# A hybrid attention and mLSTM layer in split fp32r: the mixer's key and query splits, two weight groups, the output gate's columns and the sums of weight blocks are given other places and engines

## The chip, the cores and the metric

The kernel runs on one core of a Trainium2 chip. The metric is the device time in microseconds (us) of one execution; of several executions the median is taken.

## The reference, cut to what matters

One layer on 256 tokens of width 1024, in fp32:

```python
ada = c @ w_ada + b_ada
shift, scale, gate = jnp.split(ada[:, None, :], 3, axis=-1)
h = _rmsnorm(x, norm_w) * (1 + scale) + shift
(qa, ka, va, za, qm, km, vm, zm, om, ig, fg, ga, gm) = jnp.split(h @ w_in, SPLIT_IDX, axis=-1)
...
ya = (attention(norm(qa), norm(ka), va) * silu(za)) @ w_att_proj
qm, km = jnp.split(silu(causal_dwconv(concat([qm, km]))), 2, axis=-1)
hm = mlstm(qm, km * 256 ** -0.5, vm, ig + b_igate, fg + b_fgate)
hm = sigmoid(om) * hm
hm = _rmsnorm(hm, ml_norm_w)
ym = (merge(hm) * silu(zm)) @ w_ml_proj
y = sigmoid(ga) * ya + sigmoid(gm) * ym
return x + gate * (y @ w_out)
```

The attention has 8 heads of 128, a causal mask and a relative bias. The mLSTM has 4 heads of 256. The projections qa to gm come from one weight w_in of 1024 x 11272; three more weights of 1024 x 1024 follow, and w_ada's third part gives the gate.

## The kernel before, in words

**Products.** TensorE works in fp32r, so each fp32 operand is split into a high part (a rounded copy) and a low part (what the rounding left), and each product is made three times: high by high, high by low, low by high. The weights are 112 groups, each two blocks of 128 rows by 512 columns. `split` makes a group's high part "wh" by a ScalarE copy (L506) and its low part "wl" by a VectorE subtraction (L510; eight early groups have it by GpSimd). Both lie in rings of five buffers, and group g+4 is split in the step in which TensorE multiplies group g.

**Order.** The list `place` (L354 to L366) sets the order of the groups. By number: 0-11 va, 12-19 za, 20-27 qm, 28-35 km, 36-43 w_att_proj ("att"), 44-47 ga's first half, 48-49 zm, then vm's and om's products with zm's and ga's other groups between them, 88-95 gm, 96-103 w_ml_proj ("ml"), 104-111 w_out ("out"). vm and om are made by seven products of blocks each (`PRODUCTS`, P1 P2 P5 P7 P6 P3 P4, the seven-product scheme for 2 x 2 blocks), four groups for one product of both. From P6 on the order before is: 72-75 P6, 76-77 ga's last two groups, 78-81 P3, 82-83 zm's last two groups, 84-87 P4.

**The main loop** (L1104 to L1178) goes through the groups. Step g first evacuates the block product or the "ml" chunk that ended with group g-1, then splits group g+4, then evacuates other chunks that ended, then calls what `at(step, fn)` has put on this step, and then issues the matmuls of group g (L1160 to L1177; block products L1150 to L1152). Each engine works through its own instructions in the order written, so this order decides who waits behind whom. `pump` issues loads on SP's queue into six raw buffers of 1 MB, in the order of the list `loads`, as buffers come free; the weights of the gate (`ada_gate`, four loads of 1 MB, placed by `GSEG`) are in that list, and `gate_acc` (L972) multiplies them by c on VectorE.

**Sums of weight blocks.** Some block products need sums of blocks of w_in. `block_sum` forms them in DRAM: a copy (L761) or an accumulating DMA (L763) on GpSimd's queue, or a plain one on SP's (L765), at the steps `SUM_AT`. The sums of h's blocks are VectorE's (`h_sum`, L793).

**The mixer.** `ml_split(half)` (L881) splits two heads' keys (128 x 512) and queries (128 x 1024): ScalarE copies (L889) and GpSimd subtractions (L890), at steps 44 and 47. `ml_scores` (matmuls L897 and L902, DVE L903, ACT L907, POOL L908) runs at steps 46, 47, 49, 49. `ev_block` evacuates a block product: P2 is copied, P6 has three VectorE steps (L840 to L842), P3 and P4 one (L845, L848); `block_done` then copies a finished block of vm to its high part (ACT L822) and low part (DVE L823), and a finished block of om into its place. After om's P4, two ScalarE sigmoids of 128 x 1024 (L853) finish om. `ml_num` (matmuls L919 to L921, DVE L923, ACT L924 and L926) multiplies each head by it, at steps 89 to 92; `ml_y` (DVE L934 to L937, POOL L938 to L940, DVE L945 four times) is the norm and the factor silu(zm), at 91 and 93; `ml_T` transposes (PE L956, ACT L960, DVE L961) at 94 to 97, and "ml" multiplies the result.

**The output gate.** For the last 256 of out's columns, `gate_columns` (L994) multiplies w_out itself by the gate, on GpSimd, once each at steps 99 to 102; the other columns are multiplied after the product.

Of the kernel before, what the change touches and what calls it, by code (L numbers as in the profile page):

```python
# [16 lines left out]
S = 256  # L17
# [37 lines left out]
SUM_AT = dict(vm=(5, 10, 13, 25, 21, 37, 45, 54), om=(7, 12, 16, 33, 29, 40, 50, 58))  # L55
# [16 lines left out]
def tile_hybrid(ctx: ExitStack, tc: tile.TileContext, x, c, params2, w_row, w_va, ada_mod, ada_gate,  # L72
# [282 lines left out]
    for i, ch in enumerate(chunks):  # L355
# [6 lines left out]
        for j, name in enumerate(("zm", "zm", "ga", "zm", None, "ga", "zm")):  # L362
            if name:
                place += whole[name][:2]
                del whole[name][:2]
            place += [(C[name, j], kp) for name in ("vm", "om") for kp in range(2)]  # L366
    NG = len(place)
# [67 lines left out]
    GSEG = ("qm", "qm", "ga", "zm")  # L435
# [378 lines left out]
    def block_done(name, t, n, src):  # L814
        if name == "om":
            dst = T["parts", name][t, n]
            if src is not dst:
                nc.scalar.copy(dst, src)
            return
# [5 lines left out]
    def ev_block(name, product):  # L825
# [5 lines left out]
        if product == "P1":  # L831
            nc.scalar.mul(x, a, -1.0)
# [14 lines left out]
        elif product == "P4":  # L847
            nc.vector.tensor_tensor(x, a, x, op=OP.subtract)  # L848
            block_done(name, 1, 0, x)
            if name == "om":  # L850
                for n in range(2):
                    cs = T["om"][:, :, 512 * n:512 * n + 512]
                    nc.scalar.activation(cs, cs, AF.Sigmoid)  # L853
# [27 lines left out]
    def ml_split(half):  # L881
        qm, km = T["qm"], T["km"]
        cs = slice(4 * half, 4 * half + 4)
        if half == 0:
            T["kms"] = slot("s6", [128, 2, 2, 4, 128], F32R, "kms")
        qs, ks = slot("s2", [128, 2, 4, S], F32R, "qms"), T["kms"][:, half]
        T["qms"] = qs
        for hl_, src in ((ks, km[:, cs, 0:128]), (qs, qm[:, cs])):
            nc.scalar.copy(hl_[:, 0], src)  # L889
            nc.gpsimd.tensor_tensor(hl_[:, 1], src, hl_[:, 0].bitcast(F32), op=OP.subtract)  # L890
# [98 lines left out]
    def gate_columns(kp):  # L989
# [4 lines left out]
        nc.gpsimd.tensor_tensor(w, w, T["gateb"][:, cs].unsqueeze(1).to_broadcast([128, 2, 256]), op=OP.mult)  # L994
# [52 lines left out]
    for h, step in enumerate((s + 2, s + 3, s + 5, s + 5)):  # L1047
        at(step, ml_scores, h)
    for half in range(2):
        at(s + 3 * half, ml_split, half)  # L1050
    at(start("qm") - 2, gate_init)
    gate_left = {}
    for q, s in enumerate((start("qm"), start("qm") + 2, start("att", 1), start("ga"))):
# [4 lines left out]
    at(start("gm") + 5, gate_read)  # L1058
    for q in range(4):
        at(start("ml") + 3 + q, gate_columns, q)  # L1060
# [7 lines left out]
    for q, name in enumerate(("P5", "P7", "P6", "P3")):  # L1068
        at(start("att") + 1 + 2 * q, h_sum, name)
    for q, name in enumerate(("P5", "P6", "P7", "P3")):  # L1070
        at(start("ga") + q + q // 2, h_high, name)
# [172 lines left out]
```

## Time and profile before

| what | value |
|---|---|
| median of 3 runs | 365.08 us (364.17 to 367.63) |
| the profiled execution | 366.25 us, its span 364.5 us |
| TensorE (PE) busy | 345.9 us, 95% of the span |
| VectorE (DVE) busy | 276.7 us, 76% |
| ScalarE (ACT) busy | 234.6 us, 64% |
| GpSimd (POOL) busy | 98.2 us, 27% |
| mean granted TensorE clock | 0.98 |
| DMA | 100.88 MB, mean 277 GB/s |

The profile is of one execution, and shows it from the first to the last instruction; 1.75 us lie around its span. PE busy counts modelled ends of pipelined matmuls, so a matmul that starts late is seen by its start and by the wait that stands in brackets behind it. "[2.65 <-POOL qms L890]" says that the engine sat idle for 2.65 us, until GpSimd's instruction of line 890 on the tile qms released it. In a table of windows the columns are busy time and number of instructions of PE, PE's weight loads, DVE, ACT and POOL, then the granted clock, the share of DMA and GB/s.

### The profile page before, as it was taken

Reading aid. Unit: us, or ns where it says so; the run is one execution under the profiler, and the core shown is the slowest. Engines: PE = TensorE matmul, PEld = TensorE weight load, DVE = VectorE, ACT = ScalarE, POOL = GpSimd, SP = SyncE. Lnnn points to the kernel's source line nnn. Section 1 sums busy time; section 2 is a strip of 40 time slices with the busy share of each in tenths; the row PEclk is TensorE's granted clock in tenths of the full one; section 3 lists DMA queues with packets and bytes.
Section 4 is the critical chain, followed back from the end, with each engine's and each line's share of the span. In section 5 each row is a group of like instructions: output and inputs, shape, how many; then the busy total and the mean of one; then the engine's idle time right before and its main releaser. Section 6 shows DMA issues by size and latency. Waiting matters only on the chain.

```text
span 364.5 us, 6286 instructions
## 1 busy us (share of the span) xinstructions
PE 345.9 (95%) x2408; PEld 323.6 (89%) x2408; DVE 276.7 (76%) x408; ACT 234.6 (64%) x360; POOL 98.2 (27%) x103
## 2 busy tenths in 40 slices
PE   7999999999999999999988999999999896799996
PEld 7788889999989999999988888988989895699996
DVE  4999987948965798879858685768987545778852
ACT  4768889798866876765562777765967635455410
POOL 4300004851501786568033562000000013121000
PEclk9999999999999999999998999999999999599999
DMA  8999999699999899798999949999985490072011
GB/s 268 417 414 415 416 418 373 148 414 390 304 300 260 279 350 291 289 355 227 281 299 410 341 138 290 296 377 411 420 286 206 150 369 4 0 260 88 2 58 59
DMA packets 35646, 100.88 MB, mean 277 GB/s; under 512 B 3736, under 2 KB 5664, under 8 KB 34848
## 3 DMA queue, kind: packets, MB, share of 16 engines
q1 hardware_dynamic: 30856, 87.36, 64.5%
q0 software_dynamic: 4608, 12.58, 15.3%
q10 hardware_dynamic: 152, 0.53, 0.5%
q8 instruction: 19, 0.31, 0.3%
q14 instruction: 11, 0.09, 0.1%
HBM read 99.21 MB, written 18.03 MB: 322 GB/s over the span
## 4 chain that ended last, share of the span: by engine, by line
PE 64%; issue 9%; DVE 8%; ACT 7%; POOL 6%; DMA 5%; SPq 0%; POOLq 0%; ACTq 0%; DVEq 0%
PE pm L203 12%; PE mm L1176 8%; PE mm L1177 8%; PE mm L1174 8%; DVE wl L510 3%; ACT wh L506 3%; PE mm L1160 3%; PE aux L1151 3%; PE aux L1152 3%; PE aux L1150 3%; PE mm L1169 3%; PE mm L1168 3%; PE mm L1167 3%; DMA raw<-in_w_in_dram 3%; DMA adat<-in_ada_mod_dram 2%
## 5 line engine op out<-in xcount | busy, mean ns | idle before, releaser
L510 DVE TENSOR_TENSOR wl<-raw,wh 128x1024 fp32r<-128x1024 f32 (+1 forms) x104 | 130.5, 1275 | 53.1 <-ACT wh L506 50.1
L506 ACT CAST wh<-raw 128x1024 fp32r<-128x1024 f32 (+1 forms) x112 | 111.5, 1017 | 28.9 <-PE mm L1176 10.4
L1174 PE MATMUL mm<-hTh,wh 128*128 128x256 f32 x320 | 90.4, 283 | 0.0
L1176 PE MATMUL mm<-hTl,wh 128*128 128x256 f32 x320 | 89.3, 279 | 0.0
L1177 PE MATMUL mm<-hTh,wl 128*128 128x256 f32 x320 | 89.3, 279 | 0.0
L1176 PEld LDWEIGHTS mm<-hTl,wh 128*128 128x128 f32 x320 | 60.8, 190 | 0.1
L1174 PEld LDWEIGHTS mm<-hTh,wh 128*128 128x128 f32 x320 | 60.7, 190 | 0.1
L1177 PEld LDWEIGHTS mm<-hTh,wl 128*128 128x128 f32 x320 | 60.6, 189 | 0.0
L1167 PE MATMUL mm<-wh,hTh 128*128 128x344 f32 (+1 forms) x80 | 28.0, 350 | 0.0
L1169 PE MATMUL mm<-wh,hTl 128*128 128x344 f32 (+1 forms) x80 | 27.7, 346 | 0.0
L1168 PE MATMUL mm<-wl,hTh 128*128 128x344 f32 (+1 forms) x80 | 27.7, 346 | 0.0
L188 ACT CAST wrh<-raw 128x512 fp32r<-128x512 f32 (+1 forms) x24 | 18.2, 761 | 8.5 <-DMA raw<-in_w_row_dram 8.5
L510 POOL TENSOR_TENSOR wl<-raw,wh 128x1024 fp32r<-128x1024 f32 x8 | 20.2, 2548 | 10.3 <-ACT wh L506 7.3
L938 POOL TENSOR_SCALAR f<-f 128x4 f32<-128x4 f32 x2 | 0.4, 195 | 80.4 <-DVE f L937 80.4
L193 DVE TENSOR_TENSOR wrl<-raw,wrh 128x512 fp32r<-128x512 f32 (+1 forms) x26 | 20.4, 809 | 0.9 <-ACT wrh L188 0.9
L203 PE MATMUL pm<-wrh,hTh 128*128 128x512 f32 x64 | 19.9, 392 | 0.9 <-ACT hTh L173 0.9
L1176 PE MATMUL mm<-yml,wh 128*128 128x256 f32 x64 | 19.2, 300 | 0.8 <-DVE yml L961 0.8
L203 PE MATMUL pm<-wrh,hTl 128*128 128x512 f32 x64 | 19.9, 391 | 0.0
L1174 PE MATMUL mm<-ymh,wh 128*128 128x256 f32 x64 | 19.3, 301 | 0.0
L1177 PE MATMUL mm<-ymh,wl 128*128 128x256 f32 x64 | 19.1, 298 | 0.0
L203 PE MATMUL pm<-wrl,hTh 128*128 128x512 f32 x64 | 18.9, 393 | 0.0
L1174 PE MATMUL mm<-yah,wh 128*128 128x256 f32 x64 | 17.7, 276 | 0.0
(259 smaller groups left out, 813.5 us busy)
## 6 DMA issues: line engine op xcount, KB each, us to landing
raw<-in_w_in_dram SPq DMA_DIRECT2D x30, 1024.0 KB, 12.1
adat<-in_ada_mod_dram SPq DMA_DIRECT2D x16, 512.0 KB, 8.8
raw<-in_w_va_dram SPq DMA_DIRECT2D x6, 688.0 KB, 9.7
raw<-in_ada_gate_dram SPq DMA_DIRECT2D x4, 1024.0 KB, 9.3
vm_sum<-in_w_in_dram POOLq DMA_DIRECT2D x8, 512.0 KB, 11.8
om_sum<-in_w_in_dram POOLq DMA_DIRECT2D x8, 512.0 KB, 18.2
raw<-in_w_att_proj_dram SPq DMA_DIRECT2D x4, 1024.0 KB, 8.5
raw<-vm_sum SPq DMA_DIRECT2D x8, 512.0 KB, 10.6
```

The costliest lines, as they stand in the source:

```text
L188: copy(wsp[k][0][:, c0:c1], wrow[k][:, c0:c1])
L193: e.tensor_tensor(l[:, cs], wrow[k][:, cs], h[:, cs].bitcast(F32), op=OP.subtract)
L203: nc.tensor.matmul(pm[ch][:, t], a[:, k, t * 128:(t + 1) * 128], b[:, cs], start=k == 0 and i == 0, stop=k == KT - 1 and i == 2)
L506: nc.scalar.copy(h, w)
L510: e.tensor_tensor(l, w, h.bitcast(F32), op=OP.subtract)
L1150: nc.tensor.matmul(o, a[:, k], wh[:, kk], start=ch["fresh"] and k == 0, stop=False, skip_group_check=True)
L1167: nc.tensor.matmul(o, a, wh[:, kk], start=first, stop=False)
L1168: nc.tensor.matmul(o, a, wl[:, kk], start=False, stop=False)
L1169: nc.tensor.matmul(o, b, wh[:, kk], start=False, stop=last)
L1174: nc.tensor.matmul(o, wh[:, kk, cs], sh_[:, k], start=first and i % 2 == 0, stop=False, skip_group_check=True)
L1176: nc.tensor.matmul(o, wh[:, kk, cs], sl_[:, k], start=False, stop=False, skip_group_check=True)
L1177: nc.tensor.matmul(o, wl[:, kk, cs], sh_[:, k], start=False, stop=last and i % 2 == 1, skip_group_check=True)
```

## The change

It has seven parts.

1. `ml_split` becomes `ml_keys` (ScalarE copy, GpSimd low part), called at steps 38 and 41, among att's groups, and `ml_queries` (ScalarE copy, low part by VectorE), called at 44 and 47. The scores are called at 47, 47, 49, 49.
2. In `place`, zm's last two groups go to 76-77, P3 to 78-81, P4 to 82-85, and ga's last two groups to 86-87. Thus eight groups of block products stand in a row. `done("om", 6)` is step 86; `ml_num` is at 88 to 91, `ml_y` at 90 and 92, `ml_T` at 94, 94, 96, 96.
3. Each finished block of om gets its sigmoid at once, 128 x 512 each (`block_done`), in place of a copy or nothing, and the two sigmoids of 128 x 1024 at the end go.
4. `gate_columns` runs on VectorE, a step later (100 to 103); `gate_read` a step later too.
5. `gate_acc` for the third and fourth loads is at 39-40 and 42-43 (before: 40-41 and 44-45), and the fourth of these loads stands ahead of ga's, not of zm's.
6. `SUM_AT`: the sums of weight blocks are formed one to five steps later.
7. The sums and splits of h's blocks are spread differently over the steps 40 to 51.

```diff
--- before.py
+++ after.py
@@ -52,7 +52,7 @@
             ("P6", 1, 0, False), ("P3", (1, 1), 1, False), ("P4", 3, 0, True))
 BLOCK_SUMS = ((0, (0, 0), False), (2, (0, 1), False), (0, (0, 1), True), (2, (1, 1), True), (1, 0, False),
               (1, (1, 1), True), (3, 1, False), (3, (1, 0), True))
-SUM_AT = dict(vm=(5, 10, 13, 25, 21, 37, 45, 54), om=(7, 12, 16, 33, 29, 40, 50, 58))
+SUM_AT = dict(vm=(5, 10, 18, 29, 25, 39, 48, 56), om=(7, 12, 21, 37, 33, 42, 51, 60))
 W_PIECES = ((0, 512), (512, NR), (512, 1024), (1024, NR))
 
 
@@ -359,11 +359,12 @@
             place += [(i, kp) for kp in range(4)]
             continue
         whole = {name: [(C[name, hf], kp) for hf in hfs for kp in range(4)] for name, hfs in (("zm", (0, 1)), ("ga", (1,)))}
-        for j, name in enumerate(("zm", "zm", "ga", "zm", None, "ga", "zm")):
+        for j, name in enumerate(("zm", "zm", "ga", "zm", None, "zm", None)):
             if name:
                 place += whole[name][:2]
                 del whole[name][:2]
             place += [(C[name, j], kp) for name in ("vm", "om") for kp in range(2)]
+        place += whole["ga"]
     NG = len(place)
     G0, GE_ = {}, {}
     for g, (ci, kp) in enumerate(place):
@@ -432,7 +433,7 @@
         return f
 
     NSINGLE = 3
-    GSEG = ("qm", "qm", "ga", "zm")
+    GSEG = ("qm", "qm", "ga", "ga")
     gate_loads = []
     for g, (i, kp) in enumerate(place):
         ch = chunks[i]
@@ -813,9 +814,7 @@
 
     def block_done(name, t, n, src):
         if name == "om":
-            dst = T["parts", name][t, n]
-            if src is not dst:
-                nc.scalar.copy(dst, src)
+            nc.scalar.activation(T["parts", name][t, n], src, AF.Sigmoid)
             return
         hs = slice(2 * n, 2 * n + 2)
         h = T["vm"][:, t, hs, 0:MD]
@@ -829,7 +828,7 @@
         a, b = (bk.rearrange("p (h d) -> p h d", d=MD) for bk in (T["bank", name] * 2)[:2])
         x, y, z = part[1, 0], part[1, 1], part[0, 1]
         if product == "P1":
-            nc.scalar.mul(x, a, -1.0)
+            nc.scalar.activation(x, a, AF.Copy, scale=-1.0)
         elif product == "P2":
             block_done(name, 0, 0, a)
         elif product == "P5":
@@ -847,10 +846,6 @@
         elif product == "P4":
             nc.vector.tensor_tensor(x, a, x, op=OP.subtract)
             block_done(name, 1, 0, x)
-            if name == "om":
-                for n in range(2):
-                    cs = T["om"][:, :, 512 * n:512 * n + 512]
-                    nc.scalar.activation(cs, cs, AF.Sigmoid)
 
     def ev_ga(pt, half):
         T["ga"] = T["att"]
@@ -878,16 +873,18 @@
             nc.vector.tensor_tensor(T["yl"][:, ks[q]], yf[q], T["yh"][:, ks[q]].bitcast(F32), op=OP.subtract)
 
 
-    def ml_split(half):
-        qm, km = T["qm"], T["km"]
-        cs = slice(4 * half, 4 * half + 4)
+    def ml_keys(half):
         if half == 0:
             T["kms"] = slot("s6", [128, 2, 2, 4, 128], F32R, "kms")
-        qs, ks = slot("s2", [128, 2, 4, S], F32R, "qms"), T["kms"][:, half]
+        ks, src = T["kms"][:, half], T["km"][:, 4 * half:4 * half + 4, 0:128]
+        nc.scalar.copy(ks[:, 0], src)
+        nc.gpsimd.tensor_tensor(ks[:, 1], src, ks[:, 0].bitcast(F32), op=OP.subtract)
+
+    def ml_queries(half):
+        qs, src = slot("s2", [128, 2, 4, S], F32R, "qms"), T["qm"][:, 4 * half:4 * half + 4]
         T["qms"] = qs
-        for hl_, src in ((ks, km[:, cs, 0:128]), (qs, qm[:, cs])):
-            nc.scalar.copy(hl_[:, 0], src)
-            nc.gpsimd.tensor_tensor(hl_[:, 1], src, hl_[:, 0].bitcast(F32), op=OP.subtract)
+        nc.scalar.copy(qs[:, 0], src)
+        nc.vector.tensor_tensor(qs[:, 1], src, qs[:, 0].bitcast(F32), op=OP.subtract)
 
     def ml_scores(h):
         qm, km = T["qm"], T["km"]
@@ -991,7 +988,7 @@
         li, ks, cs = raw_of[start("out", 1) + kp]
         cs = slice(cs.start + 256, cs.stop)
         w = rawt[li][:, ks, cs]
-        nc.gpsimd.tensor_tensor(w, w, T["gateb"][:, cs].unsqueeze(1).to_broadcast([128, 2, 256]), op=OP.mult)
+        nc.vector.tensor_tensor(w, w, T["gateb"][:, cs].unsqueeze(1).to_broadcast([128, 2, 256]), op=OP.mult)
 
     def ev_out(pt, c0, n, t):
         cs = slice(c0, c0 + n)
@@ -1044,20 +1041,21 @@
         at(done("za", 0) + 2 + 2 * q, att_av, 2 * q)
         at(done("za", 1) + 1 + q, att_av, 4 + 2 * q)
     s = start("ga")
-    for h, step in enumerate((s + 2, s + 3, s + 5, s + 5)):
+    for h, step in enumerate((s + 3, s + 3, s + 5, s + 5)):
         at(step, ml_scores, h)
     for half in range(2):
-        at(s + 3 * half, ml_split, half)
+        at(s - 6 + 3 * half, ml_keys, half)
+        at(s + 3 * half, ml_queries, half)
     at(start("qm") - 2, gate_init)
     gate_left = {}
-    for q, s in enumerate((start("qm"), start("qm") + 2, start("att", 1), start("ga"))):
+    for q, s in enumerate((start("qm"), start("qm") + 2, start("att") + 3, start("att") + 6)):
         at(s, gate_acc, 2 * q)
         at(s + 1, gate_acc, 2 * q + 1)
         gate_left[s + 1] = gate_loads[q]
     at(start("zm"), gate_write)
-    at(start("gm") + 5, gate_read)
+    at(start("gm") + 6, gate_read)
     for q in range(4):
-        at(start("ml") + 3 + q, gate_columns, q)
+        at(start("ml") + 4 + q, gate_columns, q)
     for name, steps in SUM_AT.items():
         for (i, src, add), step in zip(BLOCK_SUMS, steps):
             for hf in range(2):
@@ -1065,18 +1063,18 @@
     T["A"] = {}
     for kh in range(2):
         at(start("qm", 1) + 1 + 4 * kh, h_full, kh)
-    for q, name in enumerate(("P5", "P7", "P6", "P3")):
-        at(start("att") + 1 + 2 * q, h_sum, name)
-    for q, name in enumerate(("P5", "P6", "P7", "P3")):
-        at(start("ga") + q + q // 2, h_high, name)
-        at(start("ga") + q + q // 2 + 1, h_low, name)
+    for name, step in (("P5", start("att") + 4), ("P7", start("att") + 5), ("P6", start("ga") + 1), ("P3", start("ga") + 2)):
+        at(step, h_sum, name)
+    for name, step in (("P5", start("ga")), ("P7", start("ga") + 1), ("P6", start("ga") + 4), ("P3", start("ga") + 6)):
+        at(step, h_high, name)
+        at(step + 1, h_low, name)
     for hp in range(2):
         s = done("om", 6) + 2 * hp
-        at(s + 1, ml_num, 2 * hp)
-        at(s + 2, ml_num, 2 * hp + 1)
-        at(s + 3, ml_y, hp)
-        at(s + 6, ml_T, 2 * hp)
-        at(s + 7, ml_T, 2 * hp + 1)
+        at(s + 2, ml_num, 2 * hp)
+        at(s + 3, ml_num, 2 * hp + 1)
+        at(s + 4, ml_y, hp)
+        at(s + 8, ml_T, 2 * hp)
+        at(s + 8, ml_T, 2 * hp + 1)
 
     A = HB - 1
     cons = {}
```

**First place: the mixer's splits, on GpSimd and VectorE.** GpSimd's queue before (kms and qms are the keys' and queries' parts; vm_sum and om_sum the sums in DRAM; SD the scores):

```order
L763 DMA om_sum_576<-in_w_in_dram 256x1x512
L890 TENSOR_TENSOR kms<-kmT,kms 128x512
L890 TENSOR_TENSOR qms<-qmT,qms 128x1024
L761 DMA vm_sum_571<-vm_sum_567 16x8192
L908 TENSOR_TENSOR SD<-NM,SD 128x384
L761 DMA vm_sum_572<-vm_sum_568 16x8192
L908 TENSOR_TENSOR SD<-NM,SD 128x384
L890 TENSOR_TENSOR kms<-kmT,kms 128x512
L890 TENSOR_TENSOR qms<-qmT,qms 128x1024
L908 TENSOR_TENSOR SD<-NM,SD 128x384 x2
L761 DMA om_sum_579<-om_sum_575 16x8192
```

Keys and queries of a half are split here in one piece, the second half between the scores. GpSimd's queue after:

```order
L764 DMA om_sum_577<-in_w_in_dram 256x1x512
L881 TENSOR_TENSOR kms<-kmT,kms 128x512
L764 DMA om_sum_578<-in_w_in_dram 256x1x512
L764 DMA vm_sum_567<-in_w_in_dram 256x1x512
L764 DMA vm_sum_568<-in_w_in_dram 256x1x512
L881 TENSOR_TENSOR kms<-kmT,kms 128x512
L764 DMA om_sum_575<-in_w_in_dram 256x1x512
L764 DMA om_sum_576<-in_w_in_dram 256x1x512
L905 TENSOR_TENSOR SD<-NM,SD 128x384 x2
L762 DMA vm_sum_571<-vm_sum_567 16x8192
L905 TENSOR_TENSOR SD<-NM,SD 128x384 x2
```

The queries' rows are gone, and the keys' rows stand among the sums' DMAs, ahead of any score's row. VectorE's queue after, from `ml_queries` of the first half (wl are low parts of weight groups, hsum sums of h's blocks, NM the scores):

```order
L511 TENSOR_TENSOR wl<-raw,wh 128x1024
L887 TENSOR_TENSOR qms<-qmT,qms 128x1024
L511 TENSOR_TENSOR wl<-raw,wh 128x1024
L782 TENSOR_TENSOR hfull<-hfull 128x4x128
L794 TENSOR_TENSOR hsum<-hfull,hsum 128x512
L511 TENSOR_TENSOR wl<-raw,wh 128x1024
L782 TENSOR_TENSOR hfull<-hfull 128x4x128
L794 TENSOR_TENSOR hsum<-hfull,hsum 128x512
L511 TENSOR_TENSOR wl<-raw,wh 128x1024
L900 SCALAR_TENSOR_TENSOR NM<-aux,NM 128x384 x2
L887 TENSOR_TENSOR qms<-qmT,qms 128x1024
L511 TENSOR_TENSOR wl<-raw,wh 128x1024
```

The two rows of qms were in GpSimd's queue before; here each stands between the low parts of two weight groups.

**Second place: ScalarE between P3 of vm and om's last block.** Its queue before (wh are casts of weight groups; vaug is vm's finished block, mm the chunk of ga, zmt silu(zm), omt om):

```order
L858 ACTIVATE mm<-mm 128x1024
L506 CAST wh<-raw 128x1024
L822 CAST vaug<-vmt 128x2x256
L506 CAST wh<-raw 128x1024 x5
L755 ACT_TABLE_LOAD
L755 ACTIVATE zmt<-mm 128x2x512
L506 CAST wh<-raw 128x1024
L822 CAST vaug<-vmt 128x2x256
L506 CAST wh<-raw 128x1024 x2
L853 ACT_TABLE_LOAD
L853 ACTIVATE omt<-omt 128x2x512 x2
L506 CAST wh<-raw 128x1024 x2
```

Ga's sigmoid is first here, then zm's silu, and om's two long sigmoids stand last. After:

```order
L756 ACTIVATE zmt<-mm 128x2x512
L507 CAST wh<-raw 128x1024
L821 CAST vaug<-vmt 128x2x256
L507 CAST wh<-raw 128x1024 x2
L817 ACT_TABLE_LOAD
L817 ACTIVATE omt<-omt 128x512
L507 CAST wh<-raw 128x1024 x2
L821 CAST vaug<-vmt 128x2x256
L507 CAST wh<-raw 128x1024 x2
L817 ACTIVATE omt<-omt 128x512
L507 CAST wh<-raw 128x1024 x3
L853 ACTIVATE mm<-mm 128x1024
```

The long sigmoids are gone; a short one of one block of om stands behind two casts, twice (L817; one more, of P6's block, stands three casts ahead of this piece), zm's silu is first, and ga's sigmoid (L853 there) last.

**Third place: VectorE in "ml", beside out's first groups.** Its queue before (yf and yl are y and its low part):

```order
L875 TENSOR_TENSOR yf<-yf,attT 128x512
L878 TENSOR_TENSOR yl<-yf,yh 128x512 x2
L510 TENSOR_TENSOR wl<-raw,wh 128x1024 x4
L874 TENSOR_TENSOR yf<-mm,gmt 128x512
L875 TENSOR_TENSOR yf<-yf,attT 128x512
L874 TENSOR_TENSOR yf<-mm,gmt 128x512
L875 TENSOR_TENSOR yf<-yf,attT 128x512
L878 TENSOR_TENSOR yl<-yf,yh 128x512 x2
```

The low parts of four groups stand in one piece. After:

```order
L870 TENSOR_TENSOR yf<-yf,attT 128x512
L873 TENSOR_TENSOR yl<-yf,yh 128x512 x2
L511 TENSOR_TENSOR wl<-raw,wh 128x1024
L991 TENSOR_TENSOR raw<-raw,gateb 128x2x256
L511 TENSOR_TENSOR wl<-raw,wh 128x1024
L991 TENSOR_TENSOR raw<-raw,gateb 128x2x256
L511 TENSOR_TENSOR wl<-raw,wh 128x1024
L991 TENSOR_TENSOR raw<-raw,gateb 128x2x256
L511 TENSOR_TENSOR wl<-raw,wh 128x1024
L991 TENSOR_TENSOR raw<-raw,gateb 128x2x256
L869 TENSOR_TENSOR yf<-mm,gmt 128x512
```

The four rows of L991, GpSimd's L994 before, stand one behind each low part.

## What the change does to the time: a prediction

> **What bounds the kernel now.** I read the busy times first, then PE's waits, then windows of 10 us, then the timelines of the windows in which PE is not full.
>
> ```profile
> span 364.5 us, 6286 instructions
> PE 345.9 (95%) x2408; PEld 323.6 (89%) x2408; DVE 276.7 (76%) x408; ACT 234.6 (64%) x360; POOL 98.2 (27%) x103
> ```
>
> PE is the bound nearly everywhere; a change that leaves its work alone can win only what PE waits. The list of PE's waits (total, times, longest):
>
> ```profile
> PE aux L956 <- DVE omt L945: 5.1, 2, 3.8
> PE aux L902 <- POOL qms L890: 3.5, 2, 2.7
> PE aux L919 <- ACT den L924: 1.2, 1, 1.2
> PE aux L645 <- ACT GE L623: 0.8, 1, 0.8
> ```
>
> The first two are at places that the change touches. The windows tell what follows each wait (busy PE, its loads, DVE, ACT, POOL; granted clock, DMA share, GB/s):
>
> ```profile
> 190.00:200.00 10.00, 7.35 (x51) 7.20 (x50) 8.19 (x8) 3.81 (x5) 4.73 (x5) 0.83 1.05 409
> 200.00:210.00 10.00, 9.17 (x58) 8.11 (x57) 6.48 (x7) 7.22 (x9) 4.60 (x3) 1.00 0.89 329
> 210.00:220.00 10.00, 10.00 (x45) 8.28 (x45) 8.04 (x9) 7.96 (x10) 5.53 (x7) 1.00 0.55 188
> 240.00:250.00 10.00, 10.00 (x46) 8.29 (x45) 6.74 (x6) 6.62 (x8) 0.00 (x0) 1.00 1.04 409
> 280.00:290.00 10.00, 8.81 (x74) 8.57 (x74) 5.29 (x8) 7.30 (x13) 0.00 (x0) 1.00 0.24 73
> 300.00:310.00 10.00, 6.17 (x53) 5.98 (x52) 5.31 (x10) 5.36 (x13) 3.07 (x5) 0.93 0.05 19
> 310.00:320.00 10.00, 7.92 (x39) 7.35 (x40) 7.89 (x11) 4.51 (x8) 0.99 (x1) 0.55 0.00 0
> 330.00:340.00 10.00, 10.00 (x88) 10.00 (x87) 7.70 (x10) 4.92 (x6) 0.00 (x0) 1.00 0.01 3
> ```
>
> Both waits are followed by a lower clock (0.83, 0.55), so each costs more than itself. From 210 to 280 PE is full: nothing is to be won there, but something can be lost.
>
> **Part 1, keys and queries.** The scores' place:
>
> ```profile
> 185.80 1.05 ACT L506 CAST wh<-raw 128x1024 fp32r<-128x1024 f32 x1 [3.39 <-DMA raw<-in_w_in_dram]
> 188.35 2.09 POOL L890 TENSOR_TENSOR kms<-kmT,kms 128x512 fp32r<-128x512 f32 x1 [17.05 <-ACT kms L889]
> 190.41 2.35 POOL L890 TENSOR_TENSOR qms<-qmT,qms 128x1024 fp32r<-128x1024 f32 x1
> 190.72 3.11 DVE L510 TENSOR_TENSOR wl<-raw,wh 128x1024 fp32r<-128x1024 f32 x1 [1.41 <-ACT wh L506]
> 195.57 1.21 DVE L510 TENSOR_TENSOR wl<-raw,wh 128x1024 fp32r<-128x1024 f32 x1
> 189.79 0.36 PE L902 MATMUL aux<-qms,kms 128*128 128x256 f32 x1
> 192.81 1.43 PE L902 MATMUL aux<-qms,kms 128*128 128x256 f32 x5 [2.65 <-POOL qms L890]
> 195.96 0.32 PE L1174 MATMUL mm<-hTh,wh 128*128 128x256 f32 x1
> 205.91 0.86 PE L902 MATMUL aux<-qms,kms 128*128 128x256 f32 x5 [0.83 <-POOL qms L890]
> ```
>
> PE starts the second matmul 192.81 - 189.79 - 0.11 = 2.9 us late and then runs at half clock until 195.96, which loses half of 3.15, 1.5 more. In the new order the keys are split six steps earlier, so POOL's 2.09 and 2.35 are off this path; the queries' low part is a VectorE subtraction of 128x1024, 1.21 by the row of L510. It ends near 190, and the scores, one step later, are wanted at 192.1: the wait and its clock go (4.4). The second wait, where the shared buffer is read until the first two heads' scores end, falls from 0.83 to an estimated 0.4, and 0.3 of slow spacing at the first goes: 5.1 in all, of which I keep **5.0**. The row at 190.72 shows a VectorE subtraction stretched from 1.21 to 3.11 beside POOL's; the keys' two will now stretch one each among att's groups. Low parts stand well ahead of PE there (the one of 190.72 is group 49's, whose products come only after the scores of 205.91), so this costs nothing; without that cover it would cost 1.9 each.
>
> What is late next is the DMA. A cast there waits for a load:
>
> ```profile
> 241.37 1.05 ACT L506 CAST wh<-raw 128x1024 fp32r<-128x1024 f32 x1 [1.69 <-DMA raw<-om_sum]
> 242.45 1.23 DVE L510 TENSOR_TENSOR wl<-raw,wh 128x1024 fp32r<-128x1024 f32 x1 [1.51 <-ACT wh L506]
> 247.47 0.39 PE L1150 MATMUL aux<-wh,hsum 128*128 128x512 f32 x1
> ```
>
> From this low part's end (243.67) to its use are 3.8 us; a PE that is 5.0 earlier needs landings that are 1.2 earlier at least, and then has no cover left. In 200 to 220 the share is 0.89 and 0.55 since loads waited for buffers behind the stall: 1.1 + 4.5 = 5.6 us of full DMA stand free and are used when the stall goes. Part 6 brings 1 MB of om's sums into the stretch (an estimated 2.6 us at the 409 GB/s of window 190), and part 5 takes a gate load of 1 MB out of it. If these cancel, all 5.0 arrive, and that I take; if the sums cost their 2.6 and the load had been hidden, 2.4 arrive, and the range keeps that.
>
> **Parts 2 and 3, the eight block groups in a row.** The rows of now for what will stand between:
>
> ```profile
> 260.13 0.68 DVE L842 TENSOR_TENSOR omt<-omt 128x512 f32<-128x512 f32 x1
> 267.11 0.62 ACT L822 CAST vaug<-vmt 128x512 fp32r<-128x512 f32 x1 [2.74 <-DVE vmt L845]
> 267.64 4.84 ACT L506 CAST wh<-raw 128x1024 fp32r<-128x1024 f32 x5
> 272.50 1.28 ACT L755 ACT_TABLE_LOAD   x1
> 273.79 1.03 ACT L755 ACTIVATE zmt<-mm 128x1024 f32<-128x1024 f32 x1
> 276.27 0.28 PE L1174 MATMUL mm<-hTh,wh 128*128 128x256 f32 x1
> 277.64 0.62 ACT L822 CAST vaug<-vmt 128x512 fp32r<-128x512 f32 x1 [1.89 <-DVE vmt L848]
> ```
>
> The times are on the clock of before; stage 1 is taken off at the end. In the new order the sigmoid of om's P6 block stands ahead of the cast of group 80 and waits for VectorE's third step, which ends at 260.8. From there ScalarE does nine casts up to group 88's (9 x 0.97 = 8.7), two sigmoids and two vaug casts of 128x512 (0.6 each, 2.4), two table loads (2.6) and the silu (1.0): 14.7. Twice it waits for VectorE (2.74 and 1.89 now), 4.6, and a low part follows (1.2): 260.8 + 14.7 + 4.6 + 1.2 = 281.3 for group 88, which starts at 276.27 now. Setting both queues in program order by hand gives 281.9, since VectorE too falls behind; I take **281.9, 5.6 later**. Were none of the waits to occur, it would be 276.1, nothing later: the bounds are 0 and 5.6. The table loads stay as many as they were.
>
> The mixer after it:
>
> ```profile
> 297.15 1.67 DVE L945 SCALAR_TENSOR_TENSOR omt<-omt,f,zmt 128x256 f32<-128x256 f32 x4 [1.73 <-POOL f L940]
> 308.38 3.68 DVE L945 SCALAR_TENSOR_TENSOR omt<-omt,f,zmt 128x256 f32<-128x256 f32 x4 [1.70 <-POOL f L940]
> 308.33 2.66 POOL L994 TENSOR_TENSOR raw<-raw,gateb 128x512 f32<-128x512 f32 x2
> 310.02 0.45 PE L956 MATMUL aux<-ident,omt 128*128 128x128 f32 x1 [3.85 <-DVE omt L945]
> 311.72 0.90 PE L956 MATMUL aux<-ident,omt 128*128 128x128 f32 x3 [1.26 <-DVE omt L945]
> 327.74 0.28 PE L1174 MATMUL mm<-ymh,wh 128*128 128x256 f32 x1
> ```
>
> L945's second set takes 3.68 beside POOL's gate columns and 1.67 without; it ends 308.38 + 3.68 = 312.06, 35.8 after step 88 begins. In the new order every piece of the mixer stands one step nearer to step 88 (a group of 2.85 and a head's eight matmuls, some 1 us: 3.9) and the columns are gone from beside it (2.0): 35.8 - 5.9 = 29.9, so it ends at 281.9 + 29.9 = 311.8. The last transposes follow at once, in place of 311.72 with PE idle for 3.85 before. In the new order PE has spent its 5.6 already, so it arrives near 310 and waits about 1.5; then two weight groups' low parts stand ahead of yml in VectorE (2 x 1.2), and the products wait 2.1; the third group waits 1.1 for the next yml. "ml" has its second chunk at about 326.6 instead of 327.74: **1.1 won** out of all that, since the waits are moved rather than removed.
>
> I count no loss of clock for the new waits. The wait of L919, 1.2 us near 288, left the clock at 1.00 (window 280); the one of 2.65 did not, and mine are up to 2.1. Half clock for one stretch like that of 192.81 would cost 1.5, which the range holds.
>
> The Trainium skill, "TensorE: Matmul & The Clock Gate", Part 1, has the clock fall to one half only after an idle window of about 3.4 us. The row at 192.81 shows a wait of 2.65 to be enough, so the measurement decides; by the rule alone the sum would be the same, and the fourth rival below would need longer breaks than by the row.
>
> **Part 4, gate columns by VectorE.** The nearest row, two inputs in SBUF and 128x512:
>
> ```profile
> 194.96 0.68 DVE L793 TENSOR_TENSOR hsum<-hfull,hsum 128x512 fp32r<-128x512 f32 x1
> ```
>
> 4 x 0.68 = 2.7 us more on VectorE where it has 7.70 of 10 (window 330). PE is full there, with low parts some 8 us ahead, and these hide it: 0 to 0.8, taken 0.1.
>
> **Parts 5 to 7** move DMA issues on POOL's and SP's queues past each other and VectorE's small work among att's groups. None of it stands on PE's path in the rows above. One early wait, L645's of 0.8, may go or stay with the sums' DMAs that moved, which the trace of before does not tell: 0 to 0.9 with its spacing, and I take 0.5.
>
> **Sum.** 5.0 + 1.1 - 0.1 + 0.5 = 6.5. Against the profiled execution's 366.25 (span 364.5 and 1.75 around it): 359.75. The median is 365.08, 1.2 lower, which gives 358.6. Forecast: the middle, **359.2**.
>
> **Rivals.**
> - The DMA is the bound in 230 to 250 (share 1.04, casts on landings) and only 2.4 of the 5.0 arrive: 361.8. For it: the row at 241.37 and the sums that move into this stretch. Against: the free 5.6.
> - The eight groups cost little. ScalarE's two waits fall into the time in which it waits for buffers anyway; if group 88 starts 4.4 earlier than I say, everything behind it does: 354.8. For it: the bound of 276.1. Against: sigmoid and casts stand in order behind VectorE.
> - The change does not do what it says: the queries' cast stands behind the cast of group 48, which sat 3.39 for its load before. If that load is 3 us later, since the gate's fourth load is ahead of it, the queries come near 193 again, and the wait with its clock stays: 359.2 + 4.4 = 363.6.
> - Slower: the clock. It halves wherever PE breaks for more than some 2.7 us. If the break near group 84 and the one near 312 each do what the one at 310 did (clock 0.55 in 310 to 320, half speed from about 309 to 319), each costs 5 more: 369.2. It decides from a single break of 2.65; my largest is 2.1. For it: two breaks sum to 5.6 in a short stretch; against: they come in four or five pieces.
>
> **Chances.** Forecast 0.50, DMA 0.20, cheap groups 0.14, queries late 0.09, clock 0.07. The forecast's own range is 357 to 361.4. 1% of 365.08, about what a measurement of this kernel can tell from no change, ends at 361.43 and 368.73. Faster: nearly all of the forecast (0.47), the cheap groups (0.14) and the better quarter of the DMA case (0.05), 0.66. Within: the rest of these two (0.03 and 0.15), late queries (0.09), a mild clock (0.01), 0.28. Slower: 0.06. The range of 354.5 to 364.5 leaves out the clock and the tails, under 0.2.
>
> **What would show it.** Right: no wait of L902 on qms above 0.5, clock 1.00 in the windows from 185 to 205, group 49 five us earlier; new short waits of PE on wl or wh around om's P3 and P4; L956's wait on omt below 2; L945's both sets at 1.7. Wrong: casts that wait for DMA longer than 1.7 near 235 to 250 (first rival), no PE wait from P6 to gm (second), L902 still waiting over 2 (third), a clock under 0.9 in 255 to 285 (fourth).

## The result, and the profile after

The changed kernel takes 369.96 us in the median of 12 runs (367.65 to 371.63), the kernel before 365.38 (364.17 to 367.63): ratio 1.0118, 95% interval 1.0089 to 1.0146. It is slower by 4.6 us; 359.2 was forecast. The profiled execution took 367.65, the fastest of its twelve, so the traces differ by 1.4 us where the medians differ by 4.6.

The page after, and its list of PE's waits (engine, line and tile, who released it; total, times, longest):

```profile
span 365.8 us, 6273 instructions
PE 348.2 (95%) x2408; PEld 322.5 (88%) x2408; DVE 276.5 (76%) x414; ACT 234.5 (64%) x361; POOL 88.5 (24%) x97
```

```profile
PE aux L1148 <- ACT wh L507: 4.9, 2, 4.2
PE aux L1149 <- DVE wl L511: 3.0, 4, 0.8
PE mm L1174 <- DVE yml L958: 2.0, 1, 2.0
PE warm L232 <- POOL ident masks.py:199: 1.4, 1, 1.4
PE aux L953 <- DVE omt L942: 1.3, 2, 0.9
```

The two waits at which the change was aimed are gone or small: L899 (L902 before) does not appear, and L953 (L956 before) fell from 5.1 to 1.3. In their place PE waits for high and low parts of weights at block products. The scores of the first pair of heads now run without a break, and group 47 follows at once:

```profile
190.31 0.60 PE L894 MATMUL aux<-qmT,kmT 128*128 128x128 f32 x4
190.67 0.95 PE L899 MATMUL aux<-qms,kms 128*128 128x256 f32 x6
191.46 0.61 PE L894 MATMUL aux<-qmT,kmT 128*128 128x128 f32 x4
191.82 0.96 PE L899 MATMUL aux<-qms,kms 128*128 128x256 f32 x6
192.62 0.28 PE L1172 MATMUL mm<-hTh,wh 128*128 128x256 f32 x1
```

The loss starts at group 64, the first of om's P5 (the experiments' expectations call it om's P2, but P2 is groups 58 and 59; P5 is om's first product that needs a sum of weight blocks). PE, ScalarE and SP's queue there:

```profile
232.33 0.57 PE L1148 MATMUL aux<-wh,hsum 128*128 128x512 f32 x1 [4.19 <-ACT wh L507]
233.59 0.80 PE L1149 MATMUL aux<-wl,hsum 128*128 128x512 f32 x1 [0.69 <-DVE wl L511]
234.18 0.63 PE L1150 MATMUL aux<-wh,hsum 128*128 128x512 f32 x1
...
240.14 0.39 PE L1165 MATMUL mm<-wh,hTh 128*128 128x512 f32 x1
```

```profile
231.23 1.04 ACT L507 CAST wh<-raw 128x1024 fp32r<-128x1024 f32 x1 [8.04 <-DMA raw<-om_sum]
234.00 1.05 ACT L507 CAST wh<-raw 128x1024 fp32r<-128x1024 f32 x1 [1.73 <-DMA raw<-om_sum]
```

```profile
203.09 13.52 SPq L429 DMA_DIRECT2D raw<-om_sum  x2
```

PE's wait was put down to ScalarE's cast, but the cast itself had waited 8.04 us for a load of om's sums: one step further back stands the DMA. That load's two issues alone held SP's queue for 13.5 us, and its halves landed at 231.2 and 233.9; in the trace of before they were issued at 209.8 and landed at 218.2 and 219.5. After the wait the same matmuls last 0.63 instead of 0.39: the granted clock was halved until about 240 (0.66 on the mean of 230 to 240). Windows of after that tell where the DMA (share and GB/s are the last two columns) was idle and where it was full:

```profile
100.00:110.00 10.00, 10.00 (x83) 9.63 (x83) 6.68 (x19) 7.37 (x15) 0.00 (x0) 1.00 0.34 122
190.00:200.00 10.00, 10.00 (x77) 9.51 (x76) 7.45 (x8) 6.19 (x8) 2.48 (x3) 1.00 1.08 317
200.00:210.00 10.00, 10.00 (x48) 8.38 (x47) 8.45 (x9) 8.24 (x13) 4.96 (x7) 1.00 1.04 410
210.00:220.00 10.00, 10.00 (x47) 8.32 (x47) 6.46 (x7) 7.46 (x8) 1.94 (x2) 1.00 1.06 203
230.00:240.00 10.00, 6.70 (x15) 4.17 (x16) 4.16 (x4) 4.87 (x6) 0.00 (x0) 0.66 1.08 320
```

And the row of before for the first of them:

```profile
100.00:110.00 10.00, 9.22 (x76) 8.79 (x75) 5.94 (x22) 6.83 (x14) 0.00 (x0) 1.00 1.08 302
```

The DMA idled for two thirds of the window at 100 (share 0.34), where it had been full, and it was full from 190 on, where the windows at 200 and 210 had 0.89 and 0.55 before.

The start of PE's first matmul of a group, less its start in the trace of before, tells stage by stage what a kernel has won (minus) or lost. The later experiments stand in the same table (part numbers as in the section on the change). Some 0.7 to 1.0 us of each column stand already at group 8, near 72 us, ahead of anything that the change moves, so they belong to the trace of before; what counts is how a column changes downwards.

| group | place | after | part 1 only | parts 1, 4 | parts 1, 3, 4 | parts 1, 2, 4 | parts 1, 4, 2 MB less | after, 2 MB less |
|---|---|---|---|---|---|---|---|---|
| 44 | ga, before the scores | -1.85 | -0.97 | +0.92 | -0.67 | -0.75 | -0.71 | -1.53 |
| 63 | just before om's P5 | -7.25 | -6.37 | -4.16 | -6.08 | -6.07 | -6.11 | -6.94 |
| 67 | behind om's P5 | +1.53 | -6.37 | -4.16 | -6.08 | -4.45 | -6.11 | -6.43 |
| 78 | vm's P3 | +1.32 | -4.79 | -4.16 | -3.99 | -2.38 | -6.11 | -4.02 |
| 88 | gm | +8.62 | -2.84 | -2.55 | +1.21 | +2.20 | -6.12 | +5.94 |
| 100 | "ml", second chunk | +1.80 | -2.56 | -4.03 | -0.70 | -4.18 | -9.05 | -1.53 |

After wins 5.4 us between groups 44 and 63, loses 8.8 by group 67 and 7.1 more by group 88, and wins 6.8 back by group 100. In the columns with part 2, 1.1 us of the row of group 88 is no loss: the first head's numerators stand ahead of that group there and behind it in the kernel before:

```profile
283.82 0.28 PE L916 MATMUL aux<-vaug,SD 128*128 128x258 f32 x1
...
284.89 0.28 PE L1172 MATMUL mm<-hTh,wh 128*128 128x256 f32 x1
```

### The profile page after: what moved, and what is told of

It reads as the page before. It is cut to its first block, busy times and chain, and to the rows that moved or that the text cites. A ratio compares the mean times of both kernels' runs of the same rounds, so it can differ in the third digit from the quotient of the medians.

```text
span 365.8 us, 6273 instructions
## 1 busy us (share of the span) xinstructions
PE 348.2 (95%) x2408; PEld 322.5 (88%) x2408; DVE 276.5 (76%) x414; ACT 234.5 (64%) x361; POOL 88.5 (24%) x97
## 4 chain that ended last, share of the span: by engine, by line
PE 75%; DVE 7%; ACT 6%; DMA 6%; issue 3%; SPq 2%; POOL 1%; POOLq 0%; ACTq 0%; DVEq 0%
PE pm L203 12%; PE mm L1174 11%; PE mm L1172 11%; PE mm L1175 11%; DMA raw<-in_w_in_dram 6%; DVE wl L511 4%; ACT wh L507 4%; PE mm L1166 4%; PE mm L1167 4%; PE mm L1165 3%; PE mm L1158 3%; SPq L429 2%; PE aux L1148 1%; PE aux L1149 1%; PE aux L1150 1%
## 5 line engine op out<-in xcount | busy, mean ns | idle before, releaser
L511 DVE TENSOR_TENSOR wl<-raw,wh 128x1024 fp32r<-128x1024 f32 (+1 forms) x104 | 127.8, 1249 | 52.3 <-ACT wh L507 51.9
```

The source lines that it names most:

```text
L511: e.tensor_tensor(l, w, h.bitcast(F32), op=OP.subtract)
```

## The experiments

Each kernel was timed in turn with the kernel before on the same chip; ratios are to that kernel, with 95% intervals. Its median was 365.65 us in the first group (four kernels), 365.23 in the second (four), 366.58 in the third (four) and 366.49 in the last (three), so ratios are compared and not times.

### Which part loses: sums, gate, place, or part 1

**Sums back.**

```diff
-SUM_AT = dict(vm=(5, 10, 18, 29, 25, 39, 48, 56), om=(7, 12, 21, 37, 33, 42, 51, 60))
+SUM_AT = dict(vm=(5, 10, 13, 25, 21, 37, 45, 54), om=(7, 12, 16, 33, 29, 40, 50, 58))
```

> The changed kernel with the sums of weight blocks (SUM_AT) at the steps of before. In the changed profile PE has won 7.2 us by group 63, then waits 4.35 us at group 64 (om's P2) for a load of sums that was issued at 210.8 and landed at 233.9, the clock halves, and 9 us are lost by group 67. Theory A (the later copies and adds of the sums are bunched in front of that load): with the sums back, the wait at group 64 goes and most of the 9 us come back, 361 to 363 us, and no wait of PE for L507 over 1 us. Theory B (the DMA is full whatever the order of the sums, since PE asks 7 us earlier): the wait stays near 4 and the time near 369 to 370. Theory C (the loss is in the eight block groups in a row, 7 us there): 369 to 370 as well, with the wait at group 64 gone only if A holds too.

365.19 us, ratio 0.9992 (0.9966 to 1.0017). The wait at group 64 is gone and 1.26% came back, 4.6 us, less than theory A said: the second pair of scores now waits, 2.9 us by the starts of its matmuls, its queries behind a cast that waited for a load, and group 49 has 2.64 won instead of 7.25. So part 6 costs as much as the whole difference between the two kernels, and the DMA shows itself at another place. The kernel is still some 6 us above the forecast of 359.2, though, and from group 78 to 88 it loses 9.7 (-2.86 to +6.81): part 6 is not all that the forecast missed.

**Gate back.**

```diff
-    GSEG = ("qm", "qm", "ga", "ga")
+    GSEG = ("qm", "qm", "ga", "zm")
...
-    for q, s in enumerate((start("qm"), start("qm") + 2, start("att") + 3, start("att") + 6)):
+    for q, s in enumerate((start("qm"), start("qm") + 2, start("att", 1), start("ga"))):
```

> The changed kernel with the gate's third and fourth loads and their products (GSEG, gate_acc) where they were before. Theory A: this load is not what holds om's P2 back; the wait at group 64 stays over 3 us, 368 to 371 us. Theory B (DMA full before 200): the 1 MB load comes back into the full stretch, and the wait at group 64 grows by up to 2.6 us, 371 to 373 us.

369.12 us, 1.0098 (1.0070 to 1.0126): no different from the changed kernel. The late load is now zm's behind om's P5 (PE waits 5.2 us there, at 240.8). Both gate and sums back gave 366.21, 0.9988 (0.9961 to 1.0015), the same as the sums alone:

> The changed kernel with the sums' steps and the gate's loads and products (parts 5 and 6) of before. With the sums alone back 365.2 us, and PE then waits 2.9 us at the second pair of scores, behind loads that the gate's load has pushed back. Theory A2 (what counts is which transfers stand ahead of a load that PE needs): that wait goes, and 362 to 363 us come out. If the gate's load does not matter: 365 us, with the wait still there.

The second pair of scores waited there too, so the gate's load is not what delays it; part 5 moves nothing that can be measured. This kernel has parts 1 to 4 and 7, and will be compared below.

**Place back.** `place`, `ml_num`, `ml_y` and `ml_T` as before, all else changed.

> The changed kernel with the order of the groups and the mixer's steps of before (part 2 undone); the om sigmoids by block, the queries, the gate and the sums stay changed. Theory A and B: the loss at group 64 is upstream and stays; the eight groups' 7 us go, but the waits of the mixer's transposes (5 to 7 us) come back, so the sum moves by under 1.5 us: 368.5 to 371.5. Theory C: the place is what costs, and 365 or less comes out.

369.57 us, 1.0122 (1.0092 to 1.0152). With the sums back as well:

> The changed kernel with the sums and the order of the groups of before (parts 2 and 6 undone). With the sums back 365.2 us. If the eight groups in a row cost as much as the mixer's earlier steps win, as the two traces so far say (7 lost to group 88, 7 won back by group 96), 364.5 to 366 us; if the place is a loss by itself, under 363.5 us.

365.94 us, 1.0013 (0.9985 to 1.0040). Both pairs agree: as the change has it, with part 3, the place costs about what the mixer wins by it.

**Part 1 alone on the kernel before.** `ml_keys` and `ml_queries` with their steps, and the scores at 47, 47, 49, 49.

> The kernel before with part 1 alone: keys split in att by ScalarE and GpSimd, queries' low part by VectorE, scores at 47, 47, 49, 49. Theory A: no wait of the scores, full clock, 5 us won at group 49, and 2.4 to 5 of them kept to the end, 360.5 to 363 us. Theory B: the DMA takes it all back between 215 and 250, with a wait of PE for a load of sums over 3 us: 365 us or more.

363.61 us, 0.9945 (0.9924 to 0.9967). Between groups 44 and 63 it wins 5.4 us, and over half of what stood at group 63 is gone by group 88 (-6.37 to -2.84). The gain of 2.0 us (1.2 to 2.8 by the interval) is near the prediction's lower bound of 2.4, and the time is just above the 360.5 to 363 expected.

### Which of the sums, and why

**Last steps back, first steps back, third steps back.** "First" are the first that the change moved: each list's third to sixth entries; "third" is the third entry alone. In the changed kernel's `SUM_AT`:

```diff
-SUM_AT = dict(vm=(5, 10, 18, 29, 25, 39, 48, 56), om=(7, 12, 21, 37, 33, 42, 51, 60))
+SUM_AT = dict(vm=(5, 10, 18, 29, 25, 39, 45, 54), om=(7, 12, 21, 37, 33, 42, 50, 58))
...
+SUM_AT = dict(vm=(5, 10, 13, 25, 21, 37, 48, 56), om=(7, 12, 16, 33, 29, 40, 51, 60))
...
+SUM_AT = dict(vm=(5, 10, 13, 29, 25, 39, 48, 56), om=(7, 12, 16, 37, 33, 42, 51, 60))
```

> The changed kernel with only the last two steps of SUM_AT of each of vm and om back (copies and adds of the fourth sums; 45, 54 and 50, 58). Putting all sums back won 4.8 us. If the bunching of those last copies and adds (206 to 221) in front of om's P2 load is the cause, this alone brings 365 to 366.5 us and no wait at group 64. If the earlier sums that moved into 170 to 200 are the cause, 369 to 370 us.

> The counterpart: only the third to sixth steps of SUM_AT back, the last two stay late. Bunching of the last copies: 369 to 370 us, the wait at group 64 stays. Work pushed into 170 to 200: 365 to 366.5 us.

> The changed kernel with only the third step of SUM_AT of vm and om back (18 to 13, 21 to 16): the only sums that could fill the DMA near 100 us. If the idle DMA there is the cause of the wait at om's P2, the share of 100 to 110 returns to over 1 and 364.5 to 366 us come out. If it is the fourth to sixth steps that bring work into 170 to 200, 369 us or more.

Last steps back: 368.88, 1.0090 (1.0056 to 1.0124). First ones back: 364.86, 0.9974 (0.9952 to 0.9995). My first story, that the last copies and adds bunch up in front of om's P5, fell: moving them back is worth nothing clear of the noise, and the third to sixth steps are worth the rest. The third steps alone, back: 371.64, 1.0139 (1.0114 to 1.0164), so the idle time near 105 us is not it either, by itself. The windows of this last kernel show why:

```profile
100.00:110.00 10.00, 9.16 (x75) 8.72 (x74) 5.21 (x19) 7.34 (x15) 0.00 (x0) 1.00 1.07 301
140.00:150.00 10.00, 10.00 (x87) 10.00 (x86) 8.71 (x16) 6.53 (x11) 7.23 (x4) 1.00 0.33 122
```

The DMA is full again at 100 to 110 and idles at 140 to 150 instead (0.95 before): the hole has moved to the next late sums. Summing the shares of the windows from 50 to 200 gives the DMA time used by then: 14.7 windows before, 14.5 with the first sums back, 14.4 with all back, but 14.0 in the changed kernel, with the last ones back and with the third ones back. The three that are 0.4 to 0.7 windows short, 4 to 7 us of DMA, are the slow ones. The same sum over the other traces agrees: 14.0 with the gate back, with the place back and with part 6 alone, all slow, and 14.4 to 14.7 in every kernel that has all sums at the old steps. The share is a rough measure (it goes over 1), but the GB/s of the same windows say so too: 47.0 MB before, 45.3 in the changed kernel. How such a hole comes about is told by GpSimd's queue, where the third sums are issued. Before:

```profile
92.11 1.97 POOL L763 DMA_DIRECT2D vm_sum<-in_w_in_dram  x2
94.12 0.31 POOL L615 MEMSET GE<- 36x256 f32 x1
94.37 2.10 POOL L763 DMA_DIRECT2D om_sum<-in_w_in_dram  x2
```

And after:

```profile
91.25 0.31 POOL L616 MEMSET GE<- 36x256 f32 x1
110.85 1.31 POOL L709 TENSOR_TENSOR yal<-yf,yah 128x512 fp32r<-128x512 f32 x1 [19.29 <-ACT yah L708]
112.11 1.28 POOL L764 DMA_DIRECT2D vm_sum<-in_w_in_dram  x1
...
124.53 1.01 POOL L764 DMA_DIRECT2D om_sum<-in_w_in_dram  x1
```

Five steps later in the program means behind a subtraction that waits 19 us for attention's result. The four accumulating DMAs, 2 MB, start 20 to 34 us later, and nothing else fills the DMA.

**Part 6 alone on the kernel before.** The same two lines of `SUM_AT`.

> The kernel before with part 6 alone, the sums' later steps. The DMA then idles near 105 us, as in the changed kernel (share 0.34 in 100 to 110, against 1.08). If that work is missed later whatever PE's pace, om's P2 load lands near 232 as in the changed kernel, and PE, which wants it at 235 here, waits little: 365 to 367 us. If the loss comes from the sums alone, 369 to 370 us. If the sums' later steps help (the early wait of 0.9 near 105 goes), 364 us.

369.77 us, 1.0088 (1.0060 to 1.0115). PE, without the win at the scores, still loses 3.1 us from group 70 to 74 and 2 more by group 82. So the sums cost by themselves; the earlier PE of the changed kernel is not needed for it. The early wait of 0.9 near 105 does go (group 20 starts 0.9 earlier against group 12), as the prediction hoped for.

**Less to load.** The third and fourth loads of the gate's weights and their products are left out, on the changed kernel and on parts 1 and 4, so that half of the output gate is missing:

```diff
-    GSEG = ("qm", "qm", "ga", "ga")
+    GSEG = ("qm", "qm")
...
-    for q, s in enumerate((start("qm"), start("qm") + 2, start("att") + 3, start("att") + 6)):
+    for q, s in enumerate((start("qm"), start("qm") + 2)):
```

> The changed kernel without the third and fourth loads of the gate's weights and their four products, so half of the gate's vector stays zero: 2 MB less for the DMA, 4.9 us at the 410 GB/s of its full windows, and 5 us less for VectorE near 165 to 180. Theory A2 (the DMA is a second bound; the share lost at 100 to 110 is missed in 170 to 235): the wait at group 64 (4.35 and its half clock) goes for the most part, and 362 to 365 us come out. Rival (the order of issues on the queues holds om's P2 load back, not the amount): 368 to 370 us, with the wait still over 3.

> Parts 1 and 4 on the kernel before, with the same 2 MB left out. That kernel (361.7) kept 4.2 of the 5.1 us from the scores until group 80, and lost 1.5 at groups 80 to 82. If its loss is the DMA's, it goes, 359 to 360.5 us. If the DMA no longer binds there, no change: 361.7, or 0.5 less from VectorE.

364.86 us, 0.9953 (0.9927 to 0.9978), and 359.69, 0.9798 (0.9741 to 0.9855). On the changed kernel the wait at group 64 is gone (-6.94 at group 63, -6.43 at 67) with the order of all other issues untouched. On parts 1 and 4 the whole win stays up to group 88 (-6.11, -6.12). Its window behind the scores:

```profile
200.00:210.00 10.00, 10.00 (x53) 8.57 (x52) 8.50 (x9) 7.10 (x10) 5.53 (x7) 1.00 0.47 131
```

There is room again. This takes VectorE's four products away as well, which the run cannot tell apart; but the waits that went were for loads. So what holds PE from 230 on is the DMA work that is still left to do by then. Whether the order of the issues near 200 matters besides is not shown.

### The parts that can win

**Gate columns by VectorE, with part 1.**

```diff
-        nc.gpsimd.tensor_tensor(w, w, T["gateb"][:, cs].unsqueeze(1).to_broadcast([128, 2, 256]), op=OP.mult)
+        nc.vector.tensor_tensor(w, w, T["gateb"][:, cs].unsqueeze(1).to_broadcast([128, 2, 256]), op=OP.mult)
...
-        at(start("ml") + 3 + q, gate_columns, q)
+        at(start("ml") + 4 + q, gate_columns, q)
```

> The kernel before with part 1 and the gate's columns by VectorE one step later (part 4). Part 1 alone gave 363.6 us, with L945's second set still stretched beside GpSimd (3.7 against 1.7). If the stretch lies on the path, the transposes come 2 us earlier and 361.5 us comes out; the 2.7 us more on VectorE are hidden. If they are not hidden, 363.6 us or more.

361.68 us, 0.9904 (0.9867 to 0.9941), as expected (1.5 us better than part 1 alone, but the two intervals overlap). L945's second set takes 1.67 in this trace and 3.68 in that of part 1 alone.

**Om's sigmoids by block on top.** Part 3, as in the section on the change.

> The kernel before with parts 1, 3 and 4: queries by VectorE, om's sigmoids by block, gate columns by VectorE. Parts 1 and 4 alone gave 361.7 us, with PE still waiting 1.9 for the den of the first numerators behind om's two long sigmoids, and 2.2 for the last transposes. If the long sigmoids hold the mixer up, 359.5 to 361 us; if the short sigmoids between the casts cost PE as much around P6 to P4, 361.7 or more.

366.09 us, 0.9992 (0.9970 to 1.0014): not faster but 0.9% slower. ScalarE with it and, behind, without it:

```profile
253.98 1.99 ACT L506 CAST wh<-raw 128x1024 fp32r<-128x1024 f32 x2
259.38 0.63 ACT L816 ACTIVATE omt<-omt 128x512 f32<-128x512 f32 x1 [3.41 <-DVE omt L840]
259.91 2.92 ACT L506 CAST wh<-raw 128x1024 fp32r<-128x1024 f32 x3
```

```profile
253.65 4.84 ACT L506 CAST wh<-raw 128x1024 fp32r<-128x1024 f32 x5
```

ScalarE idles for 3.41 us ahead of the sigmoid of om's P6 block, which needs VectorE's three steps on that block, and three casts wait behind it that the other kernel does in one go with the two ahead. PE waits 1.87 us for the first of them, and 3.3 us are lost at groups 78 to 82 (-3.99 to +0.89, against -4.16 to -2.56 without).

**The place, without part 3.** Parts 1, 4 and 2.

> Parts 1, 4 and 2 on the kernel before: the new order of the groups and of the mixer's steps, but om's sigmoids as before, at the end. Part 3 on top of parts 1 and 4 cost 3.5 us at groups 80 to 82, where om's P6 sigmoid stands ahead of a cast. If that sigmoid is also what made the eight groups in a row dear (7 us), the mixer's earlier steps now win: 358.5 to 360.5 us. If the evacuations of vm between the casts do it, 361.7 or more.

361.53 us, 0.9865 (0.9805 to 0.9924), the lowest ratio of the kernels that compute the whole layer; its interval overlaps that of parts 1 and 4. The gain over those is smaller than expected: it loses more to loads on the way (3.7 by group 78), then 4.6 in the eight groups instead of 7.3 (3.5 and 6.2 without the numerators' 1.1), and wins 6.4 back in the mixer.

Set beside the kernel with both gate and sums back (parts 1 to 4 and 7, 0.9988), this one (parts 1, 2 and 4) is 1.23% faster, 4.5 us. So part 3, perhaps with part 7, costs about that much on the new place; on the old one part 3 alone costs 3.2 (0.9992 against 0.9904).

## Why the prediction was wrong, point by point

**The step that failed is the one on the DMA in part 1**: "Part 6 brings 1 MB of om's sums into the stretch ... and part 5 takes a gate load of 1 MB out of it. If these cancel, all 5.0 arrive." I counted one pair of sums by its new step and did not look at where the other late sums came to stand in GpSimd's queue. Parts 5 to 7 were put down with "None of it stands on PE's path". In fact the sums left 4 to 7 us of DMA unused before 200, and from 170 on the DMA is a second bound: PE had 7.25 won at group 63 and was at +1.53 at group 67. The 5.6 us of free DMA that the prediction found in 200 to 220 could cover the win at the scores or the lost time, not both; the shares there are 1.04 and 1.06 after the change. The term was -5.0 and should have been about +3.4 (-5.4 at the scores, +8.8 behind). The last bound I gave, 2.4 kept, is close to what part 1 keeps when the sums stay where they were (2.0).

**A second step failed: "stage 1 is taken off at the end", in parts 2 and 3.** It takes the cost of the eight groups to be the same for a PE that arrives earlier. Part 6 is worth 4.6 of the 10.8 us between forecast and result; with it undone 365.2 come out, not 359. The second pair of scores, which then waits for a load again, takes 2.9. The table shows another place where the rest goes: with 2 MB less to load, PE is 6.43 ahead at group 67 and still +5.94 at group 88, a loss of 11.3 without the numerators' 1.1, where the changed kernel loses 6.0. So of the 8 us that the late load cost at group 67, only 2.7 are left at group 88. What makes the stretch dear for an early PE is in part the sigmoids of part 3, 3.2 to 4.5 us by the two comparisons above; how the rest divides is open.

**The DMA rival had the place and not the size.** It took the bound as "only 2.4 of the 5.0 arrive"; it should have been a loss, from a count of the DMA's free time along the whole way.

**Part 1 was right**: no wait at the scores, full clock, 5.4 us from group 44 to 63 where 5.0 to 5.1 was forecast.

**Parts 2 and 3 came out near the forecast in the changed kernel itself, in part by luck.** Step 88 begins at 283.82 with the numerators, so from group 78 on 6.2 are lost, where 5.6 was forecast; and the mixer's 29.9 from step 88 to the end of L945 (L942 after the change) measures 313.53 - 283.82 = 29.7:

```profile
311.86 1.67 DVE L942 SCALAR_TENSOR_TENSOR omt<-omt,f,zmt 128x256 f32<-128x256 f32 x4 [1.70 <-POOL f L937]
```

```profile
310.00:320.00 10.00, 6.73 (x40) 6.17 (x39) 6.76 (x12) 4.59 (x9) 1.42 (x3) 0.73 0.16 62
320.00:330.00 10.00, 10.00 (x85) 10.00 (x83) 7.05 (x10) 5.55 (x9) 0.00 (x0) 0.93 0.56 202
```

From step 88 to group 100 the forecast was 44.7, the trace has 329.54 - 283.82 = 45.7. The wait for yml is 2.0 (2.1 forecast). The wait of 1.1 for the next yml does not occur, which makes up for about half of what the clock costs there: it halves, as the two windows show, and that was counted at nothing (see the clock rival). The cost of the eight groups is in part that of om's P6 sigmoid (4.6 without part 3 against 7.3 in the table), and it is not forced by the place.

**Part 4**: four rows of L991 of 0.68 to 0.69 each, no wait of PE behind 325, L945 at 1.67 both times. Right.

**The clock rival** happened, at a place that it did not name and at one that it did. The wait of 4.19 at group 64 halved the clock for 7 us. In the eight groups the waits are 0.5 to 0.8 each and the clock stays at 1.00. Near 312, the rival's second break, it halves from about 314.5 to 321.4: the windows at 310 and 320 have 0.73 and 0.93, and products follow each other every 0.21 us instead of 0.114, an estimated 2.4 us lost. The waits there are 0.92, 0.40 and 1.96, none as long as the single break of 2.65 from which the prediction let the clock halve, so counting no loss for breaks under that was wrong. The kernel before loses more there (about 309 to 319 at half clock).

**What stays open.** The medians differ by 4.6 us and the profiled executions by 1.4. Other kernels with late sums show the late load at om's P5 (place back, last sums back) or just behind it (gate back, third sums back, 5.2 us of waiting in each), and lose 9.6 to 11.3 us between groups 63 and 67 where the changed kernel's trace loses 8.8. So it is likely that its executions without a profile lose more there; no run shows it.

## What to carry to other kernels

When a transfer is moved later, follow its queue, not its step: what stands ahead of it there, how long that waits, and whether anything else is ready to fill the DMA meanwhile. Add up the DMA's share from the start to the place where loads become due; if it has no slack there, an idle window early on is lost time even 100 us later. An evacuation that waits for another engine must not stand ahead of casts that are ready. And before the wins of several stages are added up, ask of each later stage whether it can take what arrives earlier.

## What the runs showed of the hardware

Issuing a load can itself take long. The two loads of om's first sums held SP's queue for 13.52 us in the changed kernel, at a DMA share of 1.04 to 1.06. In the kernel before the same two took 0.80:

```profile
209.83 0.80 SPq L428 DMA_DIRECT2D raw<-om_sum  x2
```

A VectorE operation with two inputs in SBUF took 3.68 us for four beside GpSimd's multiplication of SBUF tiles and 1.67 with that gone. The Trainium skill, "SBUF — State Buffer", section "Who interferes with whom", says that a VectorE instruction with two inputs in SBUF contends with a GpSimd instruction that reads SBUF; the runs agree.

In three of the seventeen traces (the ones with the first sums back, the third sums back, and parts 1 and 4) the 128x256 products of groups 28 to 44 followed each other every 118 ns instead of 113, at a granted clock of 1.00, which cost 1.8 us there. What sets this the runs don't tell.
